# Retention's half of an output projection as seven block products instead of eight

## The chip, the cores and the metric

One core of one Trainium2 chip runs the kernel, in one launch. The metric is device time in microseconds (us) of one execution. TensorE (PE) does the matrix products, with its weight loads beside them (PEld); VectorE (DVE) and ScalarE (ACT) do the elementwise work; the queue of SyncE (SP) issues the transfers, and GpSimd (POOL) is idle in the kernel before.

## What is computed

A hybrid decoder layer over 1024 tokens of width 1024, in float32: one RMS norm and one input projection feed two groups of heads, a chunkwise retention (8 heads of 128, chunks of 128 tokens, each head normalised and gated) and a gated linear recurrence (RG-LRU). Their outputs, 1024 wide each, go through one output projection, are added to the input, and a second RMS norm follows:

```python
o_ret = group_norm_heads(chunkwise_retention(q, k, v)).reshape(B, T, RET_WIDTH)
y_ret = o_ret * jax.nn.silu(g_ret)
...
y_lru = o_lru * jax.nn.silu(g_lru)
mixed = jnp.concatenate([y_ret, y_lru], axis=-1).astype(x.dtype)
h = h + jnp.einsum('bte,ed->btd', mixed, w_out)
return rms_norm(h, norm_out_g)
```

Here T = 1024, and w_out is 2048 by 1024: its upper 1024 rows belong to retention, its lower 1024 rows to the recurrence.

## The kernel before

**Products in three parts.** Every float32 operand is split into a rounded part and a rest (`split`, L105 to L107: a cast on ACT, 128x1024, then a subtraction on DVE, 128x1024). `mm3` (L109 to L113) multiplies hi by hi, hi by lo and lo by hi, so each product of a 128x128 and a 128x512 block is three matmuls, all at L112.

**Seven products.** The input projection already forms 2x2 block products with seven block products in place of eight, from sums and differences of blocks (`combine`, L186 to L188, one DVE operation of 128x1024 for 512 KB). `NAMES` and `Parts` (L122 to L142) are its helpers.

**The output projection before.** It runs token tile by token tile (8 tiles of 128 tokens) and column half by column half (512 columns). A unit (`unit_o`, L734) is one token tile, one column half and one half of the 2048 rows: 8 row blocks, so 24 matmuls of 512 columns. The first 16 units (L887 to L907) are the recurrence's half; their results go to `hres`, together with x. The last 16 (L917 to L963) are retention's half; the very last unit of a column half runs in two cuts of 256 columns (48 matmuls of 256 columns). After the second column half, each token tile is normalised: a square with a sum on ACT (`square`, L913), then root, reciprocal and so on with one number per row, one multiplication of 128x512 on ACT (L959) and one on DVE (L961), and two stores of 256 KB.

**Retention inside it.** Retention itself is cut into 38 entries (34 pieces of work, four entries empty; `pieces`, L864, and L884 to L886) in a list `fillers`, worked off by `fill()`. A unit with fills calls it twice, after row blocks 3 and 7, so a piece stands on PE between 12 matmuls and the next 12. A piece is either scores and transposes of one chunk (L799, L806) with the transposes of the chunk before (`flip`, L859, whose result is multiplied by the gate at L861 and stored to `o_d`, L862), or state and output of a chunk (L820, L837, L838), after which statistics and normalisation run on DVE and ACT (L841 to L852) before that chunk can be flipped. 16 entries stand in the units of the recurrence's first column half, 16 in the second, and the last 6 in the first units of retention's half (L919 to L921). `load_yr` (L745) reads one token tile of `o_d` (512 KB), `slab` (L706) reads 256 rows of weights (512 KB).

**What sets the order.** Each engine works through its instructions in a fixed order that was set when the program was built; a transfer waits in SP's queue until its semaphores are there, and what stands behind it in that queue waits too.

Of the kernel before, what the change touches and what calls it, by code (L numbers as in the profile page):

```python
# [10 lines left out]
F32 = mybir.dt.float32  # L11
# [5 lines left out]
P = 128  # L17
T = 1024
# [22 lines left out]
def hybrid_layer(  # L41
# [116 lines left out]
    o_d = dram.tile([NT, P, 2, 4, P], F32, name="o_d")  # L158
# [547 lines left out]
    def slab(row, col, r=None):  # L706
        if r is None:
            r = op["wraw"].tile([P, 2, 512], F32, name="wor", tag="wor")
# [11 lines left out]
    def y_tile(src, t):  # L720

        pl = "yl" if t else "y0"
        r = op["wraw"].tile([P, NK, P], F32, name="yraw", tag="wor")
# [10 lines left out]
    def unit_o(ps, y, wg, cols, fills=True):  # L734
# [9 lines left out]

    def load_yr(t):  # L745
        yl[t] = y_tile(o_d[t].rearrange("p f h c -> p (f h) c"), t)
# [19 lines left out]
    ph_next["qkc"], ph_next["vc"] = op["qkc"], op["vc"]  # L766
# [8 lines left out]
    class Retention:  # L775
# [6 lines left out]
        def load(self, n):  # L782
            self.qk[n] = ph_next["qkc"].tile([P, 2, 512], F32, name="qkc", tag="qkc")
# [72 lines left out]
        def flip(self, n):  # L856
# [5 lines left out]
            sp.dma_start(out=o_d[n, :, self.hf].rearrange("p h c -> p (h c)"), in_=ot)  # L862
# [23 lines left out]
    fillers.extend([None, None, p_a, None, p_b] + rest)  # L886
    for dh in range(2):  # L887
        cols = slice(dh * HALF, (dh + 1) * HALF)
        w_cur = w_o
        nxt = (D, HALF) if dh == 0 else (0, 0)  # L890
        if dh == 1:
            w_o = group(*nxt, (0,))
        for t in range(NT):
            if dh == 0 and 0 < t < NT - 1:
                load_yl(t + 1)
            if dh == 0 and t == 2:
                w_o = group(*nxt, (0,))
            ps = psum()
            unit_o(ps, yl[t], w_cur, slice(0, HALF))
# [4 lines left out]
            if dh == 1 and 0 < t < NT - 2:  # L904
                load_yr(t - 1)
            if t == NT - 2:
                w_o += group(*nxt, (2, 4, 6))  # L907
# [9 lines left out]
    w_cur, w_o = w_o, group(0, HALF, (0,))  # L917
    for t in range(NT):
        if t == 4:  # L919
            while fillers:  # L920
                fill()  # L921
        if t in (0, 2, 4):
            load_yr(t // 2 + 5)
        elif t == NT - 2:
            w_o += group(0, HALF, (2, 4, 6))
        ps = psum()
        unit_o(ps, yl[t], w_cur, slice(0, HALF))
        r = hres[t][:, :HALF]
        m = ssum[:, t, 0:1]
        dve.tensor_tensor(out=r, in0=ps, in1=r, op=ALU.add)  # L930
        square(m, r)
        dve.tensor_scalar(out=m, in0=m, scalar1=1.0 / D, scalar2=EPS, op0=ALU.mult, op1=ALU.add)
        dve.tensor_tensor(out=r, in0=r, in1=gain2[:, :HALF], op=ALU.mult)
    for t in range(NT):
        r = hres[t][:, HALF:]

        mean, part = ssum[:, t, 0:1], ssum[:, t, 1:2]
        cuts = [0, HALF] if t < NT - 1 else [0, HALF // 2, HALF]
        for c0, c1_ in zip(cuts, cuts[1:]):
            ps = psum()  # L940
            unit_o(ps[:, :c1_ - c0], yl[t], w_o, slice(c0, c1_), False)
            dve.tensor_tensor(out=r[:, c0:c1_], in0=ps[:, :c1_ - c0], in1=r[:, c0:c1_], op=ALU.add)
            square(part, r[:, c0:c1_])
            if c1_ < HALF:
                dve.scalar_tensor_tensor(out=mean, in0=part, scalar=1.0 / D, in1=mean,
                                         op0=ALU.mult, op1=ALU.add)
                part = small.tile([P, 1], F32, name="part", tag="part")
# [11 lines left out]
        act.activation(out=hres[t][:, :HALF], in_=hres[t][:, :HALF], func=AF.Copy, scale=half)  # L959
        sp.dma_start(out=out[rows, :HALF], in_=hres[t][:, :HALF])  # L960
        dve.scalar_tensor_tensor(out=r, in0=r, scalar=half, in1=gain2[:, HALF:],  # L961
                                 op0=ALU.mult, op1=ALU.mult)
        sp.dma_start(out=out[rows, HALF:], in_=r)  # L963
# [69 lines left out]
```

## Time and profile before

| | us |
|---|---|
| median of 3 runs | 759.16 (757.73 to 759.18) |
| the profiled execution, its own time | 756.17 |
| its span, first to last instruction | 754.4 |
| PE busy | 731.9 (97%) |
| DVE busy | 547.8 (73%) |
| ACT busy | 414.5 (55%) |

The page divides the span into 40 slices and gives the busy share of each engine in tenths; the chain of work that ended last is followed back from the last instruction; a group of instructions shares a line, an engine, an operation and the tiles that it writes and reads. A matmul's duration in the trace is longer than its distance from the next one, because they overlap; the distance is what a matmul costs. The trace's time of landing of a transfer counts from its issue.

### The profile page before, as it was taken

The numbers are of one execution on the slowest core, as the hardware profiler recorded it, in microseconds if no ns is written. First come the engines' busy times: TensorE is split into PE (matmuls) and PEld (weight loads), VectorE is DVE, ScalarE is ACT, GpSimd is POOL, SyncE is SP. The second block draws the span as 40 slices with busy tenths as digits, with TensorE's granted clock in tenths as the row PEclk, the third lists the DMA queues.
The fourth block names the chain that finished last, engine by engine and source line by source line (L and its number), as shares of the span: only waits on it lengthen the run. The fifth ranks groups of instructions, "written<-read, shape, count | busy, mean of one in ns | idle before, by whom it ended". The sixth has DMA issues, their size and how long they took to land.

```text
span 754.4 us, 9420 instructions
## 1 busy us (share of the span) xinstructions
PE 731.9 (97%) x3508; PEld 609.9 (81%) x3508; DVE 547.8 (73%) x918; ACT 414.5 (55%) x637; POOL 0.2 (0%) x4
## 2 busy tenths in 40 slices
PE   6999999999999999999999999998999999999996
PEld 5877888887788788878788888887899988878885
DVE  6899647678877977986799988685757665662443
ACT  6795435695689679769833333245535433531332
POOL 0000000000000000000000000000000000000000
PEclk9999999999999999999999999999999999999998
DMA  9862712122213311420654444589977555413022
GB/s 305 281 200 85 251 56 71 56 90 78 70 56 112 126 57 58 138 97 29 195 139 112 113 112 112 140 248 292 310 238 250 183 182 190 160 62 120 29 86 110
DMA packets 85405, 105.58 MB, mean 140 GB/s; under 512 B 4848, under 2 KB 58224, under 8 KB 85360
## 3 DMA queue, kind: packets, MB, share of 16 engines
q1 hardware_dynamic: 85360, 104.99, 43.9%
q8 instruction: 27, 0.44, 0.2%
q14 instruction: 18, 0.15, 0.1%
HBM read 75.61 MB, written 29.36 MB: 139 GB/s over the span
## 4 chain that ended last, share of the span: by engine, by line
PE 65%; DVE 14%; ACT 10%; DMA 5%; issue 3%; SPq 1%; ACTq 0%; DVEq 0%
PE pp L112 58%; DVE xc L561 2%; PE pp L838 2%; PE pp L799 1%; PE pp L820 1%; PE pp L837 1%; DVE wq L107 1%; DVE y L614 1%; ACT wq L106 1%; DMA vc<-v_d 1%; DMA rot<-in_rot_t 1%; PE pp L859 1%; DVE wl L107 1%; ACT L643 1%; DMA graw<-in_gate_w 1%
## 5 line engine op out<-in xcount | busy, mean ns | idle before, releaser
L112 PE MATMUL pp<-wh,wq 128*128 128x512 f32 x960 | 301.5, 390 | 1.7 <-DVE cy L471 0.8
L112 PEld LDWEIGHTS pp<-wh,wq 128*128 128x128 f32 x960 | 179.9, 188 | 42.5 <-ACT cy L461 2.3
L112 PE MATMUL pp<-wl,wq 128*128 128x512 f32 x480 | 186.9, 389 | 0.0
L112 PE MATMUL pp<-wo,yt 128*128 128x512 f32 (+1 forms) x792 | 183.8, 387 | 0.0
L112 PEld LDWEIGHTS pp<-wo,yt 128*128 128x128 f32 x792 | 143.2, 188 | 27.4
L112 PEld LDWEIGHTS pp<-wl,wq 128*128 128x128 f32 x480 | 90.1, 188 | 18.6
L107 DVE TENSOR_TENSOR wq<-t,wq 128x1024 fp32r<-128x1024 f32 x40 | 48.7, 1221 | 39.1 <-ACT wq L106 32.1
L106 ACT CAST wq<-t 128x1024 fp32r<-128x1024 f32 x40 | 41.7, 1050 | 31.2 <-PE pp L112 26.6
L112 PE MATMUL pp<-wh 128*128 128x512 f32 x112 | 45.6, 407 | 8.1 <-ACT wh L106 7.9
L112 PE MATMUL pp<-wh,w 128*128 128x512 f32 x160 | 52.9, 391 | 0.1
L112 PE MATMUL pp<-wl,wh 128*128 128x512 f32 x112 | 44.8, 401 | 0.0
L112 PE MATMUL pp<-wh,wl 128*128 128x512 f32 x112 | 44.1, 398 | 0.0
L915 ACT ACTIVATE junk<-h 128x512 f32<-128x512 f32 (+1 forms) x17 | 10.3, 607 | 50.8 <-DVE h L930 26.4
L112 PEld LDWEIGHTS pp<-wh,w 128*128 128x128 f32 x160 | 30.0, 188 | 6.9 <-DVE w L107 0.6
L461 ACT COPY cy<-pp 128x512 f32<-128x512 f32 x20 | 11.6, 580 | 41.8 <-PE pp L112 41.2
L112 PEld LDWEIGHTS pp<-wh 128*128 128x128 f32 x112 | 21.7, 194 | 13.7 <-ACT wh L106 8.9
L851 ACT ACTIVATE yn<-pp,nb,rs_y 128x128 f32<-128x128 f32 x64 | 24.1, 457 | 13.2 <-DVE nb L849 13.2
L112 PE MATMUL pp<-wl,w 128*128 128x512 f32 x80 | 31.1, 389 | 0.0
L422 ACT CAST wq<-wraw 128x512 fp32r<-128x512 f32 x40 | 22.9, 616 | 9.1 <-PE pp L112 8.2
L424 DVE TENSOR_TENSOR wq<-wraw,wq 128x512 fp32r<-128x512 f32 x40 | 26.8, 681 | 0.1
L107 DVE TENSOR_TENSOR yt<-yraw,yt 128x1024 fp32r<-128x1024 f32 x16 | 19.5, 1222 | 9.1 <-ACT yt L106 9.1
L112 PEld LDWEIGHTS pp<-wl,wh 128*128 128x128 f32 x112 | 21.7, 194 | 5.2 <-DVE wl L107 0.4
(158 smaller groups left out, 1088.7 us busy)
## 6 DMA issues: line engine op xcount, KB each, us to landing
wraw<-in_w_in SPq DMA_DIRECT2D x40, 512.0 KB, 4.8
qkc<-qk_d SPq DMA_DIRECT2D x16, 512.0 KB, 6.1
wor<-in_w_out SPq DMA_DIRECT2D x14, 512.0 KB, 6.2
bt<-in_w_in SPq DMA_DIRECT2D x20, 256.0 KB, 5.4
xA<-in_xT SPq DMA_DIRECT2D x16, 256.0 KB, 5.4
v_d<-vo SPq DMA_DIRECT2D x16, 256.0 KB, 2.2
xt<-in_x SPq DMA_DIRECT2D x8, 512.0 KB, 3.4
l_d<-y SPq DMA_DIRECT2D x8, 512.0 KB, 3.1
```

The lines of the kernel that those rows point to most:

```text
L106: act.copy(out=hi, in_=src)
L107: dve.tensor_tensor(out=lo, in0=src, in1=hi.bitcast(F32), op=ALU.subtract)
L112: pe.matmul(ps, a, b, start=first and j == 0, stop=last and j == 2, skip_group_check=True)
L422: act.copy(out=h[:, j], in_=b)
L424: dve.tensor_tensor(out=l[:, j], in0=b, in1=h[:, j].bitcast(F32), op=ALU.subtract)
L461: act.copy(out=self.cy[:, :TH], in_=self.A)
L561: dve.scalar_tensor_tensor(out=xc[:, d:], in0=c[:, :T - d], scalar=cw[3 - d], in1=xc[:, d:], op0=ALU.mult, op1=ALU.add)
L614: dve.tensor_tensor_scan(out=y, data0=a, data1=y, initial=0.0, op0=ALU.mult, op1=ALU.add)
L643: act.activation(out=c, in_=c, func=AF.Silu)
L838: pe.matmul(po[:, hs], sm[:, h], vn[:, hs], start=st is None, stop=True)
L851: heads(lambda h, hs: act.activation(out=yn[:, hs], in_=po[:, hs], func=AF.Identity, scale=rs[:, h:h + 1], bias=nb[:, h:h + 1]))
L915: act.activation(out=junk[:, :src.shape[-1]], in_=src, func=AF.Square, accum_out=dst)
```

## The change

Retention's half is computed as a 2x2 block product: tokens in two halves of 512 (th), the 1024 rows of weights in two halves of 512 (kh, which is also heads 0 to 3 and heads 4 to 7) and columns in two halves of 512 (ch). Seven products P1, P2, P5, P6, P7, P3, P4 take the place of eight; each is 4 token tiles by 4 row blocks by 3 matmuls, 48 in all. Four accumulators A and four accumulators E hold sums that several products share, and each result block is added to `hres` on DVE out of them (`block_add`).

- The sums of weight blocks (two, three, two and four terms) are made by transfers: the first term is loaded by SP, the others are issued by POOL and add to the tile in place (`accum_op`). There are 14 such adding transfers of 512 KB.
- The sums and differences of retention's outputs are made on DVE (`combine`, 8 operations), and every operand is split as before.
- `o_d` is laid out by heads and tokens, so that a block of 512 tokens can be loaded; a store of 256 KB now writes runs of 512 bytes in place of 2048.
- In the second column half of the recurrence `fill()` is called after row blocks 2, 5 and 7, three times in a unit, so that all 38 entries stand ahead of retention's half.
- The last token tile's two cuts use one accumulator bank in place of two.

```diff
-    o_d = dram.tile([NT, P, 2, 4, P], F32, name="o_d")
+    o_d = dram.tile([2, 4, P, T], F32, name="o_d")
...
-            if fills and k in (3, 7):
+            if k in fills:
                 fill()
...
+    def w_load(name, pl, *blocks):
+        r = wr[name] = block(pl)
+        for i in range(2):
+            for j, (kh, ch) in enumerate(blocks):
+                src = w_out[kh * HALF + i * 256:kh * HALF + (i + 1) * 256, ch * HALF:(ch + 1) * HALF] \
+                    .rearrange("(k p) c -> p k c", p=P)
+                if j:
+                    pool.dma_start(out=r[i], in_=src, accum_op=ALU.add)
+                else:
+                    sp.dma_start(out=r[i], in_=src)
+    def w_parts(name):
+        r = wr.pop(name)
+        wt[name] = Parts(op["yl"], "yl")
+        for i in range(2):
+            wt[name].put(i, r[i])
+    def y_block(f, th):
+        ys[f, th] = block("wo" if f or th else "y0")
+        for i in range(2):
+            sp.dma_start(out=ys[f, th][i], in_=o_d[f, 2 * i:2 * i + 2, :, th * TH:(th + 1) * TH]
+                         .rearrange("h p c -> p h c"))
...
-            unit_o(ps, yl[t], w_cur, slice(0, HALF))
+            unit_o(ps, yl[t], w_cur, slice(0, HALF), (3, 7) if dh == 0 else (2, 5, 7))
...
+    def product(name, ps, t, first, last, cols=slice(0, 512)):
+        for k in range(4):
+            mm3(ps, xop[name].token(k, t), tuple(a[:, cols] for a in wt[name].row(k)),
+                first and k == 0, last and k == 3)
+    def block_add(t, th, ch, ps, op_=ALU.add, cols=slice(0, 512)):
+        r = hres[4 * th + t][:, ch * HALF + cols.start:ch * HALF + cols.stop]
+        dve.tensor_tensor(out=r, in0=r, in1=ps, op=op_)
+        return r
...
+    y_block(0, 1)
+    y_block(1, 1)
+    w_parts("P5")
+    combine(s1 := block("wo"), ys[0, 1], ys[1, 1], ALU.subtract)
+    y_parts("P5", s1)
+    for t in range(4):
+        ps = psum()
+        product("P2", ps, t, True, True)
+        block_add(t, 0, 0, ps)
+        norm_first(t, 0)
+    w_load("P6", "wraw", (0, 0), (0, 1), (1, 1))
+    w_parts("P6")
+    combine(s1, s1, ys[0, 0], ALU.subtract)
+    y_parts("P6", s1)
...
+    w_load("P4", "y0", (0, 0), (0, 1), (1, 1), (1, 0))
+    w_load("P3", "wraw", (1, 1))
...
+    for t in range(4):
+        product("P7", A[t], t, False, False)
+        block_add(t, 1, 1, A[t], ALU.subtract)
+        block_add(t, 1, 1, E[t])
+        norm_first(4 + t, 1)
+    y_parts("P4", ys[1, 1])
+    w_parts("P4")
+    for t in range(4):
+        product("P3", E[t], t, False, True)
+        r = block_add(t, 0, 1, E[t])
+        square(ssum[:, t, 1:2], r)
+        norm_last(t, 1, ssum[:, t, 1:2])
+    for t in range(4):
+        mean, part = ssum[:, 4 + t, 0:1], ssum[:, 4 + t, 1:2]
+        cuts = [0, 512] if t < 3 else [0, 256, 512]
+        for c0, c1_ in zip(cuts, cuts[1:]):
+            cols = slice(c0, c1_)
+            product("P4", A[t][:, cols], t, False, True, cols)
+            square(part, block_add(t, 1, 0, A[t][:, cols], ALU.add, cols))
...
+        norm_last(4 + t, 0, part)
```

`norm_first` and `norm_last` hold the normalisation that stood in the loops before, operation for operation.

On PE, the end of retention's pieces before (`wo,yt` are the matmuls of the units, `ident,yn` the transposes of a flip, `st` and `sm` a chunk's output):

```order
L837 MATMUL pp<-st,qkc 128x128
L838 MATMUL pp<-vc,sm 128x128
L112 MATMUL pp<-wo,yt 128x512 x24
L859 MATMUL pp<-ident,yn 128x128 x4
L112 MATMUL pp<-wo,yt 128x512 x288
L112 MATMUL pp<-wo,yt 128x256 x48
```

And now, with the same names, `qkc` for scores, and new line numbers:

```order
L112 MATMUL pp<-wo,yt 128x512 x6
L856 MATMUL pp<-ident,yn 128x128 x4
L112 MATMUL pp<-wo,yt 128x512 x9
L796 MATMUL pp<-qkc 128x128 x4
L112 MATMUL pp<-wo,yt 128x512 x3
L856 MATMUL pp<-ident,yn 128x128
L112 MATMUL pp<-wo,yt 128x512
```

The pieces stand 6 or 9 matmuls apart in place of 12, and the last two flips alternate, transpose by transpose, with single matmuls.

On DVE, one token tile of the last units before (`h<-pp,h` takes the unit's result, `v`, `half` and `root` are one number per row):

```order
L942 TENSOR_TENSOR h<-pp,h 128x512
L953 SCALAR_TENSOR_TENSOR v<-ssum 128x1
L955 RECIPROCAL half<-root 128x1
L956 SCALAR_TENSOR_TENSOR v<-v,half,root 128x1
L957 RECIPROCAL half<-v 128x1
L961 SCALAR_TENSOR_TENSOR h<-h,half,gain_5486 128x512
```

And now, on DVE, the stretch around the end of P7 (`yll_6026` is the rest part of P4's second weight block, `blk_5912` that block; `pp_5595` and `pp_5596` are of the A accumulators, `pp_5809` and `pp_5822` of the E ones; a name ending in _49 is a semaphore, DMASW those of POOL's transfers):

```order
L995 TENSOR_TENSOR h_3798<-h_3798,pp_5595 128x512 [waits PE_49]
L964 TENSOR_SCALAR ssum_5592<-ssum_5592 128x1 [waits Activation_49]
L965 TENSOR_TENSOR h_3797<-h_3797,gain2_5589 128x512 [waits DVE_49]
L995 TENSOR_TENSOR h_3798<-h_3798,pp_5809 128x512 [waits DVE_49]
L107 TENSOR_TENSOR yll_6026<-blk_5912,ylh_6024 128x1024 [waits DMASW5_49,Activation_49]
L964 TENSOR_SCALAR ssum_5592<-ssum_5592 128x1 [waits Activation_49]
L965 TENSOR_TENSOR h_3798<-h_3798,gain2_5589 128x512 [waits DVE_49]
L995 TENSOR_TENSOR h_3799<-h_3799,pp_5596 128x512 [waits PE_49]
L995 TENSOR_TENSOR h_3799<-h_3799,pp_5822 128x512 [waits DVE_49]
L995 TENSOR_TENSOR h_3792<-h_3792,pp_5783 128x512 [waits PE_49]
```

All normalisations of the last column halves stand behind the split of P4's second weight block, which waits for an adding transfer.

On POOL, which issued no transfer before, the last adding transfers (`blk_5911` and `blk_5912` are the two halves of P4's weight sum, three additions each):

```order
L901 DMA blk_5835<-in_w_out 128x2x512 [waits DMAHW7_49,DMASW1_49,DVE_49]
L901 DMA blk_5836<-in_w_out 128x2x512 [waits DMAHW0_49,DMASW3_49,DVE_49]
L901 DMA blk_5911<-in_w_out 128x2x512 [waits DMAHW1_49,DVE_49,PE_49]
L901 DMA blk_5911<-in_w_out 128x2x512 [waits DMASW0_49]
L901 DMA blk_5911<-in_w_out 128x2x512 [waits DMASW1_49]
L901 DMA blk_5912<-in_w_out 128x2x512 [waits DMAHW4_49,DVE_49,PE_49]
L901 DMA blk_5912<-in_w_out 128x2x512 [waits DMASW3_49]
L901 DMA blk_5912<-in_w_out 128x2x512 [waits DMASW5_49,DMASW4_49]
```

Each addition to a tile waits for the one before it on the same tile, and POOL issues them in this order.

## Rows read from the trace of the kernel before

**Rows 1.** The page: busy time; busy tenths in 40 slices of the span.
```profile
PE 731.9 (97%) x3508; PEld 609.9 (81%) x3508; DVE 547.8 (73%) x918; ACT 414.5 (55%) x637; POOL 0.2 (0%) x4
...
PE   6999999999999999999999999998999999999996
...
PEclk9999999999999999999999999999999999999998
```

**Rows 2.** Busy us and (instructions) by stretch: PE, PEld, DVE, ACT, POOL, clock, DMA share, GB/s.
```profile
600.00:650.00 50.00, 50.00 (x317) 44.80 (x316) 29.56 (x102) 22.72 (x56) 0.00 (x0) 1.00 0.55 184
677.00:748.00 71.00, 71.00 (x336) 59.57 (x334) 29.08 (x67) 21.06 (x46) 0.00 (x0) 1.00 0.25 86
```

**Rows 3.** The chain that ended last, from 560 us: start, us, what.
```profile
654.51 0.80 DVE stats L841 x4
...
657.12 1.51 ACT yn L851 x4
...
666.49 2.77 PE pp L112 x12
...
676.95 71.09 PE pp L112 x336
...
748.07 0.43 DVE h L942
...
750.04 0.75 DVE h L961
```

**Rows 4.** PE's only wait for another engine from 560 us on: total, times, longest.
```profile
PE pp L859 <- ACT yn L851: 1.0, 1, 1.0
```

**Rows 5.** Groups by form, PE, 680 to 740 and 742 to 747 us: busy, mean ns.
```profile
L112 PE MATMUL pp<-wo,yt 128*128 128x512 f32 x266 | 60.5, 389 | 0.0
...
L112 PE MATMUL pp<-wo,yt 128*128 128x256 f32 x41 | 5.1, 283 | 0.0
```

**Rows 6.** Groups by form on DVE and ACT, from 560 us; `bt<-bt` from 20 us.
```profile
L107 DVE TENSOR_TENSOR wo<-wor,wo 128x1024 fp32r<-128x1024 f32 x11 | 13.2, 1222 | 8.9 <-ACT wo L106 8.8
...
L106 ACT CAST wo<-wor 128x1024 fp32r<-128x1024 f32 x11 | 11.4, 1062 | 6.4 <-DMA wor<-in_w_out 6.1 <-PE pp L112 0.3
...
L930 DVE TENSOR_TENSOR h<-pp,h 128x512 f32<-128x512 f32 x8 | 5.5, 690 | 15.0 <-PE pp L112 15.0
L933 DVE TENSOR_TENSOR h<-h,gain 128x512 f32<-128x512 f32 x8 | 5.5, 682 | 0.0
...
L188 DVE TENSOR_TENSOR bt<-bt 128x1024 f32<-128x1024 f32 x8 | 9.6, 1216 | 0.0
```

**Rows 7.** DVE in order of time, one token tile: start, us, [idle before <-releaser].
```profile
731.44 0.69 DVE L942 TENSOR_TENSOR h<-pp,h 128x512 f32<-128x512 f32 x1 [2.23 <-PE pp L112]
732.92 0.16 DVE L953 SCALAR_TENSOR_TENSOR v<-ssum 128x1 f32<-128x1 f32 x1 [0.79 <-ACT junk L915]
733.25 0.16 DVE L955 RECIPROCAL half<-root 128x1 f32<-128x1 f32 x1 [0.17 <-ACT root L952]
...
733.90 0.75 DVE L961 SCALAR_TENSOR_TENSOR h<-h,half,gain 128x512 f32<-128x512 f32 x1
```

**Rows 8.** Transfers issued at 662.5, 509, 679.5, 686 and 633 us: count, KB, us to landing.
```profile
o_d<-ot SPq DMA_DIRECT2D x1, 256.0 KB, 2.0
...
qk_d<-cy SPq DMA_DIRECT2D x1, 256.0 KB, 3.2
...
yraw<-o_d SPq DMA_DIRECT2D x1, 512.0 KB, 3.4
wor<-in_w_out SPq DMA_DIRECT2D x1, 512.0 KB, 5.6
...
wor<-in_w_out SPq DMA_DIRECT2D x1, 512.0 KB, 3.7
...
wor<-in_w_out SPq DMA_DIRECT2D x2, 512.0 KB, 8.2
```

More of the change, by code (lines that the diff above doesn't have):

```diff
@@ L707, in slab @@
         if r is None:
-            r = op["wraw"].tile([P, 2, 512], F32, name="wor", tag="wor")
+            r = op["wraw"].tile([P, 2, 512], F32, name="wor", tag="wraw")
             sp.dma_start(out=r, in_=w_out[row:row + 256, col:col + 512]
@@ L722, in y_tile @@
         pl = "yl" if t else "y0"
-        r = op["wraw"].tile([P, NK, P], F32, name="yraw", tag="wor")
+        r = op["wraw"].tile([P, NK, P], F32, name="yraw", tag="wraw")
         last_load[0] = sp.dma_start(out=r, in_=src)
@@ L782, in load @@
         def load(self, n):
-            self.qk[n] = ph_next["qkc"].tile([P, 2, 512], F32, name="qkc", tag="qkc")
+            self.qk[n] = op["qkc"].tile([P, 2, 512], F32, name="qkc", tag="qkc")
             sp.dma_start(out=self.qk[n],
@@ L861, in flip @@
             dve.tensor_tensor(out=ot, in0=py, in1=self.g.pop(n), op=ALU.mult)
-            sp.dma_start(out=o_d[n, :, self.hf].rearrange("p h c -> p (h c)"), in_=ot)
+            sp.dma_start(out=o_d[self.hf, :, :, n * P:(n + 1) * P].rearrange("h p c -> p h c"),
+                         in_=ot.rearrange("p (h c) -> p h c", h=4))
     def pieces(a, b):
@@ L886, in hybrid_layer, with block, y_parts @@
     fillers.extend([None, None, p_a, None, p_b] + rest)
+    wt, ys, xop = {}, {}, {}
+    def block(pl):
+        return [op[pl].tile([P, 2, 512], F32, name="blk", tag=pl) for _ in range(2)]
+    wr = {}
+    def w_load(name, pl, *blocks):
[18 more added lines that the diff above has]
+                         .rearrange("h p c -> p h c"))
+    def y_parts(name, src):
+        pl = "qkc" if name in ("P2", "P6", "P3") else "wo" if name == "P4" else "yl"
+        xop[name] = Parts(op[pl], pl)
+        for i in range(2):
+            xop[name].put(i, src[i])
     for dh in range(2):
@@ L903, in hybrid_layer @@
             dve.tensor_tensor(out=r, in0=ps, in1=r, op=ALU.add)
[L904 to L907, printed above, removed]
+            if dh == 0 and t == NT - 2:
+                w_o += group(D, HALF, (2, 4, 6))
+            if dh == 1 and t == 2:
+                w_load("P1", "wraw", (0, 0))
+                w_parts("P1")
+            if dh == 1 and t == 4:
+                w_load("P2", "wraw", (1, 0))
+                w_parts("P2")
+            if dh == 1 and t == 5:
+                y_block(0, 0)
+                y_parts("P1", ys[0, 0])
+            if dh == 1 and t == 6:
+                y_block(1, 0)
+                w_load("P5", "wraw", (0, 0), (0, 1))
     gain2 = fin.tile([P, T], F32, name="gain2")
@@ L915, in square, with norm_first, norm_last @@
         act.activation(out=junk[:, :src.shape[-1]], in_=src, func=AF.Square, accum_out=dst)
[L917 to L930, printed above, removed]
+    def norm_first(t, ch):
+        r, m = hres[t][:, ch * HALF:(ch + 1) * HALF], ssum[:, t, 0:1]
         square(m, r)
         dve.tensor_scalar(out=m, in0=m, scalar1=1.0 / D, scalar2=EPS, op0=ALU.mult, op1=ALU.add)
[L933 to L947, printed above, removed]
+        dve.tensor_tensor(out=r, in0=r, in1=gain2[:, ch * HALF:(ch + 1) * HALF], op=ALU.mult)
+    def norm_last(t, ch, part):
+        first, last = [slice(c * HALF, (c + 1) * HALF) for c in (1 - ch, ch)]
+        mean = ssum[:, t, 0:1]
         v = small.tile([P, 1], F32, name="v", tag="v")
@@ L958, in hybrid_layer @@
         rows = slice(t * P, (t + 1) * P)
[L959 to L963, printed above, removed]
+        act.activation(out=hres[t][:, first], in_=hres[t][:, first], func=AF.Copy, scale=half)
+        sp.dma_start(out=out[rows, first], in_=hres[t][:, first])
@@ new lines, in norm_last @@
+        dve.scalar_tensor_tensor(out=hres[t][:, last], in0=hres[t][:, last], scalar=half,
+                                 in1=gain2[:, last], op0=ALU.mult, op1=ALU.mult)
+        sp.dma_start(out=out[rows, last], in_=hres[t][:, last])
+    def product(name, ps, t, first, last, cols=slice(0, 512)):
[6 more added lines that the diff above has]
+        return r
@@ new lines, in hybrid_layer @@
+    A, E = [psum() for _ in range(4)], []
+    for t in range(4):
+        product("P1", A[t], t, True, False)
+        block_add(t, 0, 0, A[t])
+        fill()
+        if t == 0:
+            y_parts("P2", ys[1, 0])
+    while fillers:
+        fill()
+    y_block(0, 1)
[8 more added lines that the diff above has]
+        norm_first(t, 0)
@@ new lines, in hybrid_layer @@
+    w_load("P6", "wraw", (0, 0), (0, 1), (1, 1))
[3 more added lines that the diff above has]
+    for t in range(4):
+        E.append(psum())
+        product("P5", E[t], t, True, False)
+    w_load("P7", "wraw", (0, 1), (1, 1))
+    w_parts("P7")
+    s3 = ys[0, 1]
+    combine(s3, ys[0, 0], s3, ALU.subtract)
+    y_parts("P7", s3)
+    for t in range(4):
+        product("P6", A[t], t, False, False)
+        block_add(t, 0, 1, A[t], ALU.subtract)
+    w_load("P4", "y0", (0, 0), (0, 1), (1, 1), (1, 0))
@@ new lines, in hybrid_layer @@
+    w_load("P3", "wraw", (1, 1))
+    w_parts("P3")
+    s4 = ys[1, 0]
+    combine(s4, s1, s4, ALU.add)
+    y_parts("P3", s4)
+    for t in range(4):
+        product("P7", A[t], t, False, False)
[4 more added lines that the diff above has]
+    w_parts("P4")
+    for t in range(4):
+        product("P3", E[t], t, False, True)
+        r = block_add(t, 0, 1, E[t])
+        square(ssum[:, t, 1:2], r)
+        norm_last(t, 1, ssum[:, t, 1:2])
@@ new lines, in hybrid_layer @@
+    for t in range(4):
+        mean, part = ssum[:, 4 + t, 0:1], ssum[:, 4 + t, 1:2]
[4 more added lines that the diff above has]
+            square(part, block_add(t, 1, 0, A[t][:, cols], ALU.add, cols))
+            if c1_ < 512:
+                dve.scalar_tensor_tensor(out=mean, in0=part, scalar=1.0 / D, in1=mean,
+                                         op0=ALU.mult, op1=ALU.add)
+                part = small.tile([P, 1], F32, name="part", tag="part")
+        norm_last(4 + t, 0, part)
```

11 lines of the change are left out of this document (3 added, 8 removed).

## The prediction

> **What bounds the kernel now.** I read the page's busy shares first, then its slices, then the windows of the last 200 us, then the chain. PE is busy 97% of the span, at 9 tenths or more in nearly every slice, and its granted clock is at the higher level (2.4 GHz) until the last slice [rows 1]; from 600 to 748 us it shows no gap worth naming, while DVE is busy 59% in one stretch and 41% in the next, ACT less [rows 2]. The chain is PE's: 336 matmuls in a row end at 748.04 us, and only then DVE's and ACT's last token tile follows, up to 750.79 us, and its stores, up to the span's end at 754.4 [rows 3]. PE's one wait for another engine in this part is 1.0 us, for ACT's normalised chunk ahead of a flip [rows 4]. So matmuls taken out are worth their distance, as long as what feeds and empties PE keeps up. That is the question, since the change moves work to DVE, ACT and a new queue.
>
> **Matmuls.** 266 matmuls of 512 columns take 60.5 us, 0.227 us each; 41 of 256 take 5.1, 0.12 each [rows 5]. Retention's half has 16 units of 24 now, the last of them as 48 of half the width: 360 and 48. Seven products of 48, the last token tile as 24 of half the width, are 324 and 24: minus 36 x 0.227 and 24 x 0.12, **-11.1 us**. The retention pieces themselves stay. The wait of 1.0 us at the last flips has matmuls to fill it now, since transposes and single matmuls alternate: **-1.0**. Seven more changes between units and pieces: a block of 12 between pieces takes 2.77 us against 12 x 0.227 = 2.73 [rows 3], so **+0.2** in all. PE alone would then end at 748.04 - 11.9 = 736.1 us.
>
> **DVE after the recurrence's half.** Call zero the end of the last of its matmuls. From there PE has 324 x 0.227 + 24 x 0.12 = 76.6 us of work, so zero is at 659.5 us. DVE has, up to the last addition of P7 (read from the order): 20 splits and 8 combinations of 128x1024 at 1.22, 21 additions out of accumulators at 0.69, 7 multiplications by the gain at 0.68, 7 small ones at 0.16 [rows 6, 7]: 24.4 + 9.8 + 14.5 + 4.8 + 1.1 = 54.6 us. Before, DVE had 29 us of work in 71 [rows 2]; now it has little slack. It can't start on this at once: P5's difference needs the last token block of both halves, and that needs the last flip, which stands two matmuls ahead of zero. From there: the gate's multiplication 0.7 (a 128x512 operation), then the store, then the load. The store now has 512-byte runs: 3.2 us, as the store of that form to `qk_d`, against 2.0 in long runs [rows 8]. The load of 512 KB takes 3.4 alone and 5.6 with others [rows 8]; it has a weight block beside it, so I take 4.5. With 0.3 for the queue that is 8.7 us, and DVE has done 3.3 us of other work by then: 5.4 of waiting. So DVE ends that part at 54.6 + 5.4 = 60.0. PE ends P7 at 240 x 0.227 = 54.5 and wants the last E bank, which DVE empties last, for the fourth tile of P3 at 62.7: PE isn't held yet, and the order puts the operands of each product some microseconds ahead of it.
>
> Then DVE is the bound. A token tile's normalisation holds DVE from its addition at 731.44 to the end of L961 at 734.65: 3.2 us, 1.1 of it waits for ACT [rows 7]. Before, a tile came every 24 x 0.227 = 5.5 us; in P3 and P4 one comes every 12 x 0.227 = 2.7. Seven tiles at 3.2 make 22.5; the order pulls two additions into such waits, -1.4; two leftovers of the fourth tile, +0.85. The last tile in cuts, from its addition to the end, is 2.75 as now (748.04 to 750.79) [rows 3]. Sum: 60.0 + 22.5 - 1.4 + 0.85 + 2.75 = 84.7. By PE alone it would be 76.6 + 2.75 = 79.4. **+5.3 us**.
>
> **Splits on ACT** (1.06 us each [rows 6]) run ahead of DVE's halves and add nothing: 20 of them in 60 us. **The denser pieces**: output to flip has at the least 6 + 9 matmuls and another piece, above 5 us, while the way from the statistics at 654.51 to the end of the four normalisations at 658.63 took 4.1 [rows 3]. So nothing; if splits of the new weight blocks come between them on DVE, the 1.0 us of now [rows 4] once per late flip, twice at most. **The queues**: SP's loads of the last token block stand behind P6's second weight block, whose buffer comes free with DVE's first split after zero; that is 2 us after zero, ahead of the store's landing, so nothing.
>
> **The adding transfers.** The trace before has none, and POOL issues none. Two ends from the nearest rows: 3.4 us, a plain load of 512 KB alone, if the addition is free; 7.4, twice a load of 3.7 [rows 8], if the tile's own bytes are read as a second transfer. In a crowd a load took 8.2 [rows 8]. The tightest chain is P4's. Its first tile is the buffer of a token block that DVE has read for the last time some 21 us after zero; SP's load lands 3.5 later, at 24.5; two additions follow in turn before POOL gets to the second tile, which needs three: 24.5 + 5 X. DVE wants it at about 55.5, and ACT's cast 1.1 ahead: X up to 5.9 us costs nothing, and each microsecond above costs 5, since the split stands in DVE's queue ahead of every normalisation. The other additions have more room (P6's second block, loaded by about 6, has two in turn and DVE wants it at 25: 9 us each). Between 3.4 and 7.4 I take 5.4, half way, nearer to the load of 512 KB among others (5.6) than to either end: **0**.
>
> The Trainium skill's Collectives: The Full Stack (The bandwidth ceiling: the fold count and why AG ≠ RS ≠ AR) says that an adding transfer costs no cycles for the addition but reads two sources, and moves about half as many bytes in a time as a copy, 31 GB/s per engine for copies. By it 512 KB over 16 engines at half of that would be an estimated 2.1 us, and with the 2.0 us of fixed time that DMA: Bandwidth & Descriptors (Anatomy of one DMA — SWDGE (gpsimd) path) gives for POOL's queue, 4.1 us: below the 5.9, so the sum stays. No row here shows it.
>
> **The sum.** -11.1 - 1.0 + 0.2 + 5.3 = -6.6 us on the profiled 756.17, so 749.6; the median of the runs lies 3.0 above that execution, so **753 us**.
>
> **The rivals.**
> *The additions are slow.* At X of 7.2 us the 5 x (X - 5.9) has eaten 6.5 us; from there the kernel is slower. At 7.4, the upper end, 760; at 8.6, 766. For it: every addition waits for the landing of the one before, and three or five of them stand in a row; the crowd's 8.2. Against: after zero nearly nothing else is in flight. 0.27. Between 5.9 and 7.2, 753 to 759.5: 0.13.
> *DVE isn't the bound.* If its waits for ACT overlap better than now and the token block lands early, PE's end counts: 753 - 5.3 = 748. For it: DVE's sum has 10 us of waits in it. Against: one fixed order, and each wait there is a round trip of one tile. 0.10.
> *As summed*, 749 to 757: 0.50.
> That PE does not lose the 36 matmuls is excluded by the order, which shows them gone.
>
> **How the numbers follow.** Likeliest: 753, by itself 749 to 757. Below 748 I leave 0.08, above 766 0.11. A measurement of this kernel can tell about 0.2% (1.5 us) from no change. Faster: 0.48 of the 0.50, 0.10, and 0.06 of the 0.13: 0.64. Within: the other 0.02 of the likeliest (late flips) and 0.06 of the 0.13: 0.08. Slower: the 0.27 and the last 0.01: 0.28.
>
> **What would show it.** Right: PE's busy time falls by about 11 us; DVE is at 8 tenths or more from about 668 us to the end; in the last 25 us PE waits for DVE (the last cut for the emptying of its bank, about 4 us); the chain's end is DVE and ACT with normalisations. POOL's transfers land within 5.9 us of each other. Wrong: DVE stands still at the splits of weight sums with the releaser a POOL transfer, in P7's time above all; or PE waits ahead of P5 or P6 for operands; or gaps on PE ahead of flips.

## The result and the profile after

The changed kernel takes 770.65 us (median of 4 runs, 768.49 to 771.76); the kernel before took 758.44 on the same chip. The ratio is 1.0166, with a 95% interval of 1.0146 to 1.0186: 1.7% slower, some 12 us. The forecast was 753 us, 748 to 766: the sign is wrong and the time lies outside the range. The profiled execution took 770.49 us; its span is 768.7.

First the page of the changed kernel: busy time, and busy tenths in 40 slices of 19.2 us.

```profile
PE 729.0 (95%) x3448; PEld 604.5 (79%) x3448; DVE 575.8 (75%) x950; ACT 426.2 (55%) x649; POOL 17.4 (2%) x18
...
PE   6989999999999999999999999997999999999764
...
PEclk9999999999999999999999999999999999999987
```

Against [rows 1], PE has the 60 matmuls less, but the last three slices fall to 7, 6 and 4 tenths, and in the last two the granted clock falls too. The same in three stretches (columns as in [rows 2]; the stretches begin at the end of the recurrence's half):

```profile
664.00:718.00 54.00, 54.00 (x240) 44.63 (x238) 39.59 (x47) 19.40 (x26) 8.52 (x7) 1.00 0.71 161
718.00:745.00 27.00, 14.75 (x52) 11.38 (x51) 14.00 (x27) 8.27 (x18) 3.66 (x3) 0.81 0.40 68
745.00:769.00 24.00, 12.39 (x60) 10.50 (x58) 13.57 (x43) 11.18 (x28) 0.00 (x0) 0.75 0.45 165
```

Up to 718 PE has no gap. From 718 to 745 it is busy 14.75 of 27 us, DVE 14.00, ACT 8.27: none of them bounds this stretch. What they wait for, from 600 us on (total, times, longest):

```profile
POOL blk L901 <- DMA blk<-in_w_out: 61.0, 8, 16.7
ACT ylh L106 <- DMA blk<-in_w_out: 28.8, 5, 10.4
...
PE pp L112 <- DVE h L995: 17.0, 3, 6.9
...
DVE yll L107 <- ACT ylh L106: 11.2, 5, 9.7
...
DVE qkcl L107 <- ACT qkch L106: 9.3, 2, 9.1
```

Read from the second line down: ACT's cast of a weight block waits for a transfer into `blk`, DVE's split waits for that cast, and PE waits for DVE's additions, which stand in DVE's queue behind the split. The chain that ended last has the same in order of time (start, us, what):

```profile
724.23 1.21 POOL blk L901
...
730.24 5.67 DMA blk<-in_w_out
735.99 1.05 ACT ylh L106
737.07 1.22 DVE yll L107
738.36 0.60 DVE h L965
```

The last two additions of P4, then cast and split, then the normalisations of the last column halves, as the order of DVE ahead of the prediction says. POOL in order of time, from P6's second block on (start, us, [idle before <-releaser]):

```profile
670.84 1.21 POOL L901 DMA_DIRECT2D blk<-in_w_out  x1 [16.71 <-DMA blk<-in_w_out]
679.31 1.22 POOL L901 DMA_DIRECT2D blk<-in_w_out  x1 [7.26 <-DMA blk<-in_w_out]
685.24 1.21 POOL L901 DMA_DIRECT2D blk<-in_w_out  x1 [4.71 <-DVE h L995]
691.23 1.22 POOL L901 DMA_DIRECT2D blk<-in_w_out  x1 [4.77 <-DVE qkcl L107]
697.28 1.21 POOL L901 DMA_DIRECT2D blk<-in_w_out  x1 [4.83 <-PE pp L112]
706.00 1.22 POOL L901 DMA_DIRECT2D blk<-in_w_out  x1 [7.50 <-DMA blk<-in_w_out]
712.10 1.21 POOL L901 DMA_DIRECT2D blk<-in_w_out  x1 [4.88 <-DMA blk<-in_w_out]
718.18 1.22 POOL L901 DMA_DIRECT2D blk<-in_w_out  x1 [4.87 <-issue]
...
730.24 1.22 POOL L901 DMA_DIRECT2D blk<-in_w_out  x1 [4.80 <-DMA blk<-in_w_out]
```

Ten additions: P6's second tile twice, P7's two tiles once each, P4's first tile three times, its second three times. Seven of the nine distances are 5.9 to 6.1 us, also where the tile is another one and nothing in the program makes it wait: the row at 718.18 is the first addition to P4's second tile, SP's last load had landed by 704.3 (issued at 697.2, at most 7.1 us to landing), and the releaser is "issue", nothing that the profile shows. It comes 0.3 us after the landing of the addition before, which was to the other tile. So the additions stand in one line of 65 us, from 670.8 to 735.9. That is theory one. The rivals: each waits for its own tile alone, as the prediction had it, and something else made them late; or the end of DVE's normalisations and the lower clock are the bulk of the loss.

### The profile page after: what moved, and what is told of

It reads as the page before. It is cut to its first block, busy times and chain, and to the rows that moved or that the text cites. A ratio compares the mean times of both kernels' runs of the same rounds, so it can differ in the third digit from the quotient of the medians.

```text
span 768.7 us, 9387 instructions
## 1 busy us (share of the span) xinstructions
PE 729.0 (95%) x3448; PEld 604.5 (79%) x3448; DVE 575.8 (75%) x950; ACT 426.2 (55%) x649; POOL 17.4 (2%) x18
## 4 chain that ended last, share of the span: by engine, by line
PE 59%; ACT 14%; DVE 13%; DMA 7%; issue 5%; SPq 1%; POOL 0%; ACTq 0%; DVEq 0%; POOLq 0%
PE pp L112 51%; PE pp L796 2%; PE pp L835 2%; PE pp L834 2%; DMA bt<-in_w_in 1%; DVE xc L561 1%; PE pp L817 1%; DVE wq L107 1%; DVE y L614 1%; PE pp L856 1%; DMA xt<-in_x 1%; ACT wq L106 1%; DMA graw<-in_gate_w 1%; DMA vc<-v_d 1%; ACT L601 1%
## 5 line engine op out<-in xcount | busy, mean ns | idle before, releaser
L112 PE MATMUL pp<-wo,yt 128*128 128x512 f32 x384 | 97.9, 402 | 0.0
L112 PEld LDWEIGHTS pp<-wo,yt 128*128 128x128 f32 x384 | 70.4, 191 | 13.0
L106 ACT CAST ylh<-blk 128x1024 fp32r<-128x1024 f32 x20 | 20.5, 1049 | 43.2 <-DMA blk<-in_w_out 28.8
L901 POOL DMA_DIRECT2D blk<-in_w_out x14 | 17.2, 1228 | 713.8 <-DVE ot L858 622.6
L107 DVE TENSOR_TENSOR yll<-blk,ylh 128x1024 fp32r<-128x1024 f32 x20 | 24.1, 1221 | 11.3 <-ACT ylh L106 11.2
L112 PE MATMUL pp<-ylh,qkch 128*128 128x512 f32 x48 | 20.3, 422 | 12.3 <-DVE h L995 12.3
```

What stands on the lines that cost most here:

```text
L106: act.copy(out=hi, in_=src)
L107: dve.tensor_tensor(out=lo, in0=src, in1=hi.bitcast(F32), op=ALU.subtract)
L112: pe.matmul(ps, a, b, start=first and j == 0, stop=last and j == 2, skip_group_check=True)
L901: pool.dma_start(out=r[i], in_=src, accum_op=ALU.add)
```

## The experiments

### Without the additions

```diff
-                if j:
-                    pool.dma_start(out=r[i], in_=src, accum_op=ALU.add)
-                else:
+                if not j:
                     sp.dma_start(out=r[i], in_=src)
```

> The changed kernel with its 14 adding transfers left out: each sum of weight blocks is its first term alone, so POOL issues nothing; all other work stays. Theory one (the additions stand in one line on POOL, ten of them from 670.8 to 735.9 us, and DVE and ACT stand behind the last two): without them DVE ends at the end of the recurrence's half, 663.7, plus the 84.7 of the prediction = 748.4 in place of 764.9; 16.5 us less than the changed kernel, about 754 us. Rival (the end of DVE's normalisations at 3.1 us a tile and TensorE's lower granted clock after its pauses make most of it, and would be there anyway): 6 us less at the most, 764 us or more.

Measured: 748.6 us, ratio 0.9881 (0.984 to 0.9921). Windows and, below, the end of its chain:

```profile
664.00:718.00 54.00, 54.00 (x240) 44.72 (x239) 47.02 (x59) 23.88 (x34) 0.00 (x0) 1.00 0.31 93
718.00:745.00 27.00, 22.12 (x108) 18.45 (x106) 19.85 (x57) 14.61 (x37) 0.00 (x0) 0.98 0.37 137
```

```profile
717.50 1.23 DVE yll L107
...
739.77 1.70 PE pp L112 x12
...
743.48 0.75 DVE h L982
```

The split that began at 737.07 begins at 717.50, 19.6 us earlier, and DVE ends at 744.2 in place of 764.9. The time is 5 us below the expected 754, because DVE's end was costed too long (see the account of the sum below). The second rival falls: the end of the normalisations is there and costs little. The first, that an addition waits for its own tile alone, isn't tested by this run, since nothing is left to wait for. In per cent of the kernel before, the additions cost 1.0166 - 0.9881 = 2.85%, 21.6 us. The products themselves bring 1.2%.

### Copies in place of additions

```diff
-                    pool.dma_start(out=r[i], in_=src, accum_op=ALU.add)
+                    pool.dma_start(out=r[i], in_=src)
```

> The 14 transfers of POOL copy in place of adding (the addition is left out; same tiles, same order, same waits). If the addition itself is what takes long: each lands in 2 to 4.5 us and is issued so much sooner, the line of ten is at most 45 us in place of 65, its last lands by 716, and the time comes to that without additions, about 754 us. If POOL's line is what takes long, whatever the transfer does: 5.5 to 6.1 us from issue to issue, and 768 to 771 us.

Measured: 751.67 us, ratio 0.9915 (0.9889 to 0.9941), near the time without additions and below the 754 expected. POOL in order of time:

```profile
701.81 1.50 POOL L901 DMA_DIRECT2D blk<-in_w_out  x2 [5.58 <-DMA blk<-in_w_out]
707.82 0.72 POOL L901 DMA_DIRECT2D blk<-in_w_out  x1 [4.51 <-DMA blk<-in_w_out]
712.45 0.72 POOL L901 DMA_DIRECT2D blk<-in_w_out  x1 [3.90 <-DMA blk<-in_w_out]
```

Two things differ from the additions. At 701.81 two copies, the last to P4's first tile and the first to its second, are issued one right behind the other (x2), so more than one is in flight. And the distance on one tile, 707.82 to 712.45, is 4.6 us where additions had 6.1. So POOL isn't held to 6 us a transfer whatever the transfer does; on one tile an addition takes 1.4 us more than a copy from issue to issue, and in the changed kernel no addition had another beside it.

### P4's additions in turns

```diff
+        order = [(i, j) for i in range(2) for j in range(len(blocks))]
+        if name == "P4":
+            order.sort(key=lambda o: o[1])
-        for i in range(2):
-            for j, (kh, ch) in enumerate(blocks):
+        for i, j in order:
...
+                    with tc.issue_after(adds[-1].ins) if adds else nullcontext():
+                        adds.append(pool.dma_start(out=r[i], in_=src, accum_op=ALU.add))
```

> Only the order on POOL is changed for P4's weight sum: first, second and third addition of the two tiles in turns (tile 0, tile 1, tile 0, ...) in place of three to the one and then three to the other. If POOL has one transfer in flight whatever its tile: still 6.1 us from issue to issue, the last of the six lands at about 736 as now, the last of tile 0 only at 730 (now 717.8), and the time is 769 to 775 us. If a transfer waits only for the addition before it on its own tile (as the prediction had it): pairs are issued 1.2 to 2 us apart, the six take some 20 us in place of 38, the last lands by 722, and the time falls by 10 us or more, to 760 or less.

Measured: 774.22 us, ratio 1.0227 (1.0184 to 1.027).

```profile
705.46 1.22 POOL L905 DMA_DIRECT2D blk<-in_w_out  x1 [8.11 <-DVE h L999]
711.44 1.22 POOL L905 DMA_DIRECT2D blk<-in_w_out  x1 [4.75 <-issue]
...
730.09 1.22 POOL L905 DMA_DIRECT2D blk<-in_w_out  x1 [5.07 <-issue]
```

And on DVE:

```profile
731.87 1.23 DVE L107 TENSOR_TENSOR qkcl<-blk,qkch 128x1024 fp32r<-128x1024 f32 x1 [22.27 <-ACT qkch L106]
```

P4's last five. Neighbours go to different tiles, and still they stand 6.0 to 6.3 us apart, from 705.46 to 730.09; their releaser is nothing that the profile shows. The chain of one tile, on which the prediction reckoned, is not what binds, and the first rival falls. The kernel is slower than the changed kernel because of P4's first tile: its third addition, now the fifth of six, lands at 729.8 in place of 717.8. ACT's cast of that tile waits for it, the cast of `qkch` stands behind on ACT, and DVE waits 22.3 us for that one, where it waited 9.1 in the changed kernel.

### Room for one, room for two

What holds the next addition back while one is in flight? The kernel sets aside 1024 bytes of each partition of SBUF for the descriptors of POOL's transfers. The next kernels set aside 64 bytes more.

```diff
-    nc = bacc.Bacc("TRN2", target_bir_lowering=False, num_devices=1, dynamic_dma_scratch_size=1024)
+    nc = bacc.Bacc("TRN2", target_bir_lowering=False, num_devices=1, dynamic_dma_scratch_size=1088)
```

On top of the turns:

> P4's additions in turns, as in p4_in_turns (774.2 us), and the part of SBUF that is set aside for the descriptors of POOL's transfers raised from 1024 to 1088 bytes a partition, all that is left. If room for descriptors is what keeps POOL at one addition in flight (copies: three), and two additions need only a little more than there is: additions to the two tiles are issued 1.2 to 3 us apart and the last lands by 725; about 760 us. If two need much more than that, or if room isn't the reason: 6.1 us from issue to issue as before, 774 us.

On the changed kernel as it is:

> The changed kernel with one number changed: 1088 bytes a partition in place of 1024 for the descriptors of POOL's transfers; the order of the additions is the changed kernel's own. Theory (room for one addition in flight makes the line; 64 bytes more are room for two): additions to different tiles that follow one another overlap (second of P6 with first of P7, P7's two, P7's last with P4's first, P4's third with fourth), additions to one tile still follow one another at 6.1 us. Four of the nine distances in the line of ten fall from 6.1 to some 1.5 to 4 us: 10 to 15 us less, the last lands at 720 to 726 in place of 735.9, and the time is 755 to 761. If the gain of room_1088 came from turns and room together only: 768 or more.

Measured: 759.61 us (ratio 1.003, 1.001 to 1.005) with the turns, against 774.22 without the 64 bytes; 763.18 (1.0062, 1.0039 to 1.0085) without the turns, against 770.65. POOL, with the turns, P4's last five:

```profile
701.29 2.47 POOL L905 DMA_DIRECT2D blk<-in_w_out  x2 [9.45 <-PE pp L112]
707.49 1.22 POOL L905 DMA_DIRECT2D blk<-in_w_out  x1 [3.73 <-DMA blk<-in_w_out]
...
713.64 1.21 POOL L905 DMA_DIRECT2D blk<-in_w_out  x1 [2.29 <-DMA blk<-in_w_out]
```

```profile
717.91 1.23 DVE L107 TENSOR_TENSOR qkcl<-blk,qkch 128x1024 fp32r<-128x1024 f32 x1 [8.20 <-ACT qkch L106]
```

At 701.29 two additions, to one tile and to the other, go out together (x2), and the five take 18.2 us to the last landing (719.5) where they took 30.4. One number of the program, 6% more room, is worth 8 us without the turns and 15 with them, by the ratios. What still parts the turns from the 748.6 us without additions stands, for the most part, at the first tile again: its third addition (issued at 710.13) lands at 715.8, and DVE waits 8.2 us there, the second line above. Without the turns the time is 2 us above the 755 to 761 expected: of the four distances that were to shrink only two did clearly, to 4.4 and 1.2 us; three additions that had another beside them took 8 to 9.5 us to land, and P4's last three, all to one tile, still wait for each other's landing.

The same limit from the other side, with the old 1024 bytes, turns, and each addition in two halves:

```diff
-                        adds.append(pool.dma_start(out=r[i], in_=src, accum_op=ALU.add))
+                    for k in range(2):
...
+                            adds.append(pool.dma_start(out=r[i][:, k], in_=src[:, k], accum_op=ALU.add))
```

> As p4_in_turns (774.2 us, one addition of 512 KB in flight), each addition cut into two of 256 KB; room stays 1024 bytes. If room for descriptors sets how much is in flight: two or three halves fly at once, the second half is issued 1 to 1.6 us after the first, a pair takes 6 to 7 us, and with turns the next tile's half starts as soon as one has landed: the last lands by 725 to 735, 762 to 772 us. If POOL allows one adding transfer at a time whatever its size: each half takes 4 us or more (about 2 us of fixed part and half of the rest), a line of twenty in place of ten, 80 us or more, and 785 us or more.

Measured: 762.84 us, ratio 1.0072 (1.0042 to 1.0102).

```profile
708.36 2.68 POOL L906 DMA_DIRECT2D blk<-in_w_out  x3 [9.35 <-PE pp L112]
712.37 0.86 POOL L906 DMA_DIRECT2D blk<-in_w_out  x1 [1.33 <-issue]
```

Three halves go out at once (x3), the fourth when one has landed. So it is room that holds the next one back, and room is not counted one by one.

What it is counted in, the packets of POOL's queue suggest. First 14 additions, then 14 copies of the same bytes, then 28 half additions (packets, MB, share of the engines):

```profile
q0 software_dynamic: 3808, 7.34, 6.1%
...
q0 software_dynamic: 2016, 7.34, 3.2%
...
q0 software_dynamic: 4032, 7.34, 6.0%
```

That is 272 packets for an addition and 144 for a copy or a half addition. With 1024 bytes, one addition (272), three halves or three copies (432; the copies from DRAM to DRAM in the last section) were in flight, never two additions (544); with 1088 bytes, two. All of it fits a room counted in packets which, with 1024 bytes, is an estimated 432 to 543. No run tests this apart from the sizes.

### Denser pieces alone

```diff
-            unit_o(ps, yl[t], w_cur, slice(0, HALF))
+            unit_o(ps, yl[t], w_cur, slice(0, HALF), (3, 7) if dh == 0 else (2, 5, 7))
```

> The kernel before with one part of the change: three pieces of retention in a unit of the recurrence's second column half (after row blocks 2, 5 and 7) in place of two. As the prediction had it (each output has 5 us to its flip, and DVE keeps up): 0 to 1 us more, 757 to 759 us. If denser pieces are what made the recurrence's half end 4.2 us later than predicted (663.7 in place of 659.5 us): 3 to 4 us more, about 761.

Measured: 758.31 us, ratio 1.0007 (0.9988 to 1.0025). This part of the change costs nothing that can be measured.

### The sums made early, in DRAM

```diff
+    w_d = {n: [dram.tile([P, 2, 512], F32, name=f"w_d{n}{i}") for i in range(2)] for n in ('P5', 'P6', 'P7', 'P4')}
...
+        if name in w_d:
+            for i in range(2):
+                sp.dma_start(out=r[i], in_=w_d[name][i])
+            return
...
     v_phase()
+    w_sums()
```

`w_sums` issues on POOL, term by term over the eight tiles, a copy for the first term and an addition for each further one.

> The same eight tiles of weight sums are made by POOL in DRAM, from about 100 us on (8 copies and 14 additions), and SP loads them at the places where it loaded the first terms. All else as in the changed kernel. Theory one: 22 transfers of 6.1 us end by 240 us, far ahead of their use at 602; the tail is that without additions: about 754 us, 0.5% below the kernel before. Rival (normalisations and clock): 764 us or more. What would spoil it: transfers from 100 to 240 us that delay the input projection's loads; the chain would show it there.

Measured: 752.43 us, ratio 0.9947 (0.9916 to 0.9978): the 754 expected, and faster than the kernel before. But 3.8 us of the gain of 748.6 are missing, and the trace has them ahead of the output projection. So the transfers were moved:

```diff
     v_phase()
-    w_sums()
...
+        if run.i == 6:
+            w_sums(run.q[5].cx)
         run.step()
```

> As sums_early (752.4 us), but POOL begins its 22 transfers at about 205 to 215 us in place of 77, behind the sixth group of columns of the input projection. sums_early lost 4 us against no_additions ahead of the output projection (its first matmul at 500.0 in place of 495.3 us), at TensorE's waits at 96, 130 and 200 us. If these waits came from POOL's transfers beside the projection's loads: they are gone, about 748.6 us, as without additions. If the transfers cost as much wherever they stand: 752.

Measured: 755.75 us, ratio 0.9969 (0.9947 to 0.9991), above both of the expected values. The loss went with the transfers. Waits from 205 to 340 us, first of this kernel, then of the kernel before:

```profile
PE pp L112 <- ACT gw L106: 6.2, 2, 3.6
...
ACT gw L106 <- DMA graw<-in_gate_w: 5.8, 2, 3.0
```

```profile
PE pp L112 <- ACT gw L106: 0.8, 2, 0.6
```

Two loads of the gates' weights, 3.1 us from issue to landing in the kernel before, take 5.4 and 6.3 beside POOL's transfers, and PE waits for both. Neither of the two places tried for these 11.5 MB of transfers was free, though the DMA share in them was only 0.30 and 0.28 in the kernel before (0.76 and 0.72 with the transfers).

### One sum that grows

P6's sum is P5's and one block more, P4's is P6's and one block more. So one pair of tiles can hold all three in turn: 8 additions in place of 14, with six in the line in place of ten.

```diff
-    w_load("P6", "wraw", (0, 0), (0, 1), (1, 1))
+    w_more("P6", w_sum, 1, 1)
...
-    w_load("P7", "wraw", (0, 1), (1, 1))
+    w_load("P7", "wo", (0, 1), (1, 1))
...
-    w_load("P4", "y0", (0, 0), (0, 1), (1, 1), (1, 0))
-    w_load("P3", "wraw", (1, 1))
+    w_more("P4", w_sum, 1, 0)
+    w_load("P3", "y0", (1, 1))
```

Here `w_sum` is P5's pair of tiles, and `w_more` issues one addition to each of the two.

> One sum of weight blocks grows in place: P5's (two terms) gets P6's third term added once P5's split has read it, and that one P4's fourth, in place of three sums from nothing. 8 additions in place of 14, 2 first loads less; P7's sum stands in two tiles of another pool, P3's block in those that were P4's. Room stays 1024 bytes. Theory one: the line on POOL is then P6's two, P7's two and P4's two from 665 to 671 on, at 6.1 us each; the last lands by about 706, ahead of its use at 717.5, so nothing waits and the time is that without additions, about 748.6 to 750 (1% below the kernel before). If the split that an addition waits for now comes so late that operands come late: waits of TensorE ahead of P6 (696) or P4 (729), 752 or more.

Measured: 751.27 us, ratio 0.9899 (0.9869 to 0.9928), some 1 us above the expected. POOL after the recurrence's half:

```profile
666.98 1.21 POOL L910 DMA_DIRECT2D blk<-in_w_out  x1 [32.12 <-DVE yll L107]
677.36 1.23 POOL L910 DMA_DIRECT2D blk<-in_w_out  x1 [9.16 <-DVE yll L107]
683.48 1.21 POOL L901 DMA_DIRECT2D blk<-in_w_out  x1 [4.90 <-issue]
...
705.09 1.22 POOL L910 DMA_DIRECT2D blk<-in_w_out  x1 [6.40 <-DVE h L1002]
```

Six in all, 7.6 us apart on average and never two at once, but the last lands at about 711, ahead of its split at 718.5, and PE waits for no other engine from 664 until its last cut. This keeps nearly the whole gain of the products, the additions are still made by transfers, and it is 1% faster than the kernel before.

### The normalisations in step

In two kernels DVE took the next token tile's addition ahead of the rest of the normalisation before it:

```diff
-        norm_last(t, 1, ssum[:, t, 1:2])
+        if rest:
+            with tc.issue_after(last_add[0].ins):
+                rest()
+        rest = norm_last(t, 1, ssum[:, t, 1:2])
```

> As sums_from_210, and in P3 and P4 DVE takes the addition of the next token tile ahead of the rest of the normalisation of the one before, which now doesn't stand between them. Without additions the last seven tiles took 19.2 us on DVE from 722.3 on, TensorE waited 1.6 us at the end, and DVE ended 2.75 us after it. If DVE's end is the bound there (theory one with the prediction's DVE term, cut to what was measured): TensorE's 1.6 us go, so 747 us. If not: the same as sums_from_210.

> As sum_grown, with DVE's addition of the next token tile ahead of the rest of the normalisation before, in P3 and P4. If DVE's chain of normalisations still holds TensorE at the end (1.6 us without additions): 1 to 1.6 us less than sum_grown. If, as in sums_from_210_in_step, it doesn't: the same within 0.5 us.

Measured: 755.94 (ratio 0.9975, 0.9951 to 0.9998) beside 755.75, and 749.79 (0.9878, 0.985 to 0.9906) beside 751.27. The first pair says nothing was gained, the second points to 1.5 us, and the intervals of each pair overlap. PE's wait ahead of the last cut was 1.3 us long without it and 1.1 with it, in both pairs: at most a small part of the forecast's 5.3 is there to be won.

## Why the prediction was wrong

**The step that failed is the adding transfers.** Its duration was a small part of that. X was taken as 5.4 with 5.9 as the limit; alone it measured 6.05 from issue to issue, 0.15 over the limit, which at 5 X would cost 0.8 us. What was wrong is "24.5 + 5 X" itself. It followed P4's tiles alone and let an addition wait only for the one before on the same tile. Put by that formula on the measured end of the recurrence's half, 663.7, with the measured X, P4's second tile lands at 663.7 + 24.5 + 5 x 6.05 = 718.5. It landed at 735.9, 17.4 us later, from three parts that the rows of POOL show:

- P4's first addition went out at 697.3 in place of 688.2: 9.1 us, because the second addition of P6's second block and P7's two stood in the same line ahead of it. The prediction named P6's block as one that "has more room" and didn't put it into P4's sum.
- The first addition to the second tile doesn't overlap with the third to the first, as the formula had it: six X in place of five, 6.05 us.
- The first of the six, beside two of SP's loads, took 8.7 us: 2.7 more than X. The last counts only to its landing, 5.6: 0.4 less.

Then "the split stands in DVE's queue ahead of every normalisation" was right, and the price with it. DVE had been held once before: P4's first tile, at 717.8 in place of the 706.4 that the formula gives it, made DVE wait 9.1 us for a cast that stands on ACT behind that tile's; the second tile made it wait 9.7 more. DVE ended 20.7 us later than without additions: 19.6 at the second split, and some 1.2 at the very end, where PE's last cut of 12 matmuls took 2.94 us in place of 1.70. There the granted clock had fallen, behind a wait of 4.8 us:

```profile
750.00:757.00 7.00, 4.46 (x26) 3.75 (x24) 4.55 (x15) 4.07 (x11) 0.00 (x0) 1.00 0.55 204
757.00:765.00 8.00, 2.93 (x12) 2.63 (x12) 5.32 (x18) 4.17 (x11) 0.00 (x0) 0.51 0.41 151
```

0.51 is the lower level (1.2 GHz). Behind the two longer waits before it fell too (0.57 from 723.6 to 727 us, 0.50 from 740.3 to 742); DVE waits nowhere for PE between 737 and 762 us, so there this cost nothing that is seen.

The rival "the additions are slow" had the right place, sign and releasers, with 0.27. It was priced by X, up to 7.4 or 8.6 us, where the count in the line was what mattered: 65 us for ten, with X at 6.05. "Against: after zero nearly nothing else is in flight" was no argument, since the line needs nobody else.

**The estimate for one addition.** The Trainium skill's Collectives: The Full Stack (The bandwidth ceiling: the fold count and why AG ≠ RS ≠ AR), which measures reductions between cores, gave an estimate of 4.1 us for an addition, below the limit. The trace has 5.6 to 5.8 from issue to landing, alone, and 4.2 for a copy of the same bytes. The Trainium skill's DMA: Bandwidth & Descriptors (SWDGE vs HWDGE vs iDMA) says that the descriptors of POOL's transfers stand in rings in a part of SBUF. The runs agree with that, by the 64 bytes; how many transfers such a part holds is told by the runs alone.

**The rest of the sum, on the kernel without additions.** Its span is 748.0; the sum had 754.4 - 6.6 = 747.8. That agreement is luck, since two terms missed and cancelled:

- "Zero" came at 663.4 in place of 659.5. In these traces 3.1 of the 3.9 us are PE's wait for a load of `qkc` at 520 us, with what follows: 4.3 us long in this trace, 3.9 in the changed kernel, 3.8 with the denser pieces alone, 2.7 in the one trace of before; and behind the longer wait the granted clock fell here too (0.86 from 518 to 530 us in the changed kernel, 1.00 before), and the next 24 matmuls of its chain took 6.0 us in place of 4.35. With the denser pieces alone PE came to that wait 2.6 us earlier, and the span was that of before (754.2): what the longer wait costs on the whole stays open, since before has one trace. The gain of 1.0 at the late flips was also not there (0.4 of waiting is left).
- DVE's end was 3.9 shorter than the 84.7. Up to the last work of P7 it needed 58.8 us, not 60.0 (its waits up to the token block came to 4.3 us where 5.4 were put). The seven token tiles took 19.2 us, not 21.95: as on the chain at 723 to 736, a tile takes 3.1 on its own, and 2.4 where the next addition fell into its wait. So DVE's bound costs 1.5 us and not 5.3, and "DVE isn't the bound" (748) was nearly right.
- The **denser pieces** were costed at 0 and measured at 0.0007 of the time; the 60 matmuls are gone as counted.
- The **3.0 us** between the profiled execution and the median have no cause in the sum, and without additions the median lies 1.2 below the profiled execution (748.6 and 749.77).

**What would show it.** The sign for "wrong" was named and came: DVE stands still at the splits of weight sums, at the end of P7 and just after it, with a transfer of POOL behind it. The sign for "right", "POOL's transfers land within 5.9 us of each other", looked at the pace of the line and not at its length. The sign "PE's busy time falls by about 11 us" came with 2.9 (731.9 to 729.0), and with 8.7 without additions (723.2): a matmul of 512 columns at the lower clock is busy for 0.63 us and not 0.39, so busy time doesn't count matmuls.

## What to carry to other kernels

Cost a queue as a queue: list everything that an engine issues in its order, assume that nothing overlaps until a row shows that it does, and start the chain at the queue's first busy moment, not at the buffer that the last item needs. Where POOL issues large transfers, its room for descriptors is a resource like any buffer: look for an issue whose releaser is nothing that the profile shows and that follows a landing by 0.3 us. And when several sums share terms, let one grow in place: it took four of the ten links out of the line and turned a loss of 1.7% into a gain of 1%.

## What the runs showed of the hardware

- An adding transfer of 512 KB to SBUF lands 5.6 to 5.8 us after its issue when it is alone, a copy of POOL after 4.2; POOL itself is busy 1.22 us with an addition and 0.72 with a copy.
- With 1024 bytes a partition for descriptors, one such addition was in flight at a time and three of half the size; with 1088 bytes, two whole ones. In the packets of POOL's queue an addition of 512 KB is 272, a copy of the same bytes or a half addition 144.
- Additions from DRAM to DRAM, 14 behind 8 copies, took 6.1 to 9.1 us each, one at a time too; the copies went three at a time:

```profile
76.73 2.23 POOL L178 DMA_DIRECT2D w_dP<-in_w_out  x3
85.86 0.66 POOL L178 DMA_DIRECT2D w_dP<-in_w_out  x1 [6.90 <-issue]
...
101.29 1.06 POOL L176 DMA_DIRECT2D w_dP<-in_w_out  x1 [4.48 <-issue]
109.61 1.07 POOL L176 DMA_DIRECT2D w_dP<-in_w_out  x1 [7.27 <-issue]
```
